# Cross-attention scores of a two-block decoder: one float32 product against three float32r products of high and low halves

## The chip, the core and the metric

The kernel runs on one core of one Trainium2 chip. The metric is the device time of one execution in microseconds (us). Work is spread over TensorE (PE: matmuls, and PEld for its weight loads), VectorE (DVE), ScalarE (ACT), GpSimd (POOL) and SyncE (SP), which issues the transfers. Each engine runs its own list of instructions in order and waits on semaphores for the others.

## The reference

256 tokens of width 1024 pass through two blocks. The first has two layers; each is a mixer (an mLSTM in the first layer, stick-breaking attention in the second), a cross-attention into 256 memory tokens and a SwiGLU network. The second block mixes three branches (hgrn, forgetting attention, attention into a second memory) and ends in a gated network with a convolution. All of it is float32. The part that the change touches is this, once in each layer:

```python
def memory_cross_attention(h, mem_n, w_q, w_kv, w_o):
    q = (h @ w_q).reshape(B, S, XA_HEADS, XA_HEAD_DIM)            # 4 heads of 256
    kv = (mem_n @ w_kv).reshape(B, mem_n.shape[1], 2, XA_HEADS, XA_HEAD_DIM)
    k, v = kv[:, :, 0], kv[:, :, 1]
    s = jnp.einsum('bthd,bmhd->bhtm', q, k).astype(jnp.float32) * (XA_HEAD_DIM ** -0.5)
    p = jax.nn.softmax(s, axis=-1).astype(v.dtype)
    o = jnp.einsum('bhtm,bmhd->bthd', p, v).reshape(B, S, D_MODEL)
    return o @ w_o
```

Two other parts of the reference play a role below. The second block normalises its memory keys by head (`kh = _rmsnorm(mk.reshape(B, M, MEM_HEADS, MEM_DH), k_g)`), and its hgrn branch needs causal masks over chunks of 64 tokens.

## The kernel before, in words

The 256 tokens are two halves h of 128 rows. Every projection (`project`, `project_T`) is already done as three float32r products: the weights are split into a high and a low half (`split_weight`: L211 on ACT casts the high half, L212 on DVE subtracts it from the raw weights to get the low half), the activations likewise (`split`: L364 on ACT, L365 on DVE), and the products hi·hi, hi·lo and lo·hi are added in PSUM (L240, L241, L244 in `prod`; L317 to L322 in `project_T`).

The cross-attention is `xattn`. Its query projection makes four blocks (h, b), h a half and b a pair of heads. Each starts a chain of its own: scale the block (L812), transpose it on PE (L354) and copy it back with the factor 1/16 on DVE (`to_T`, L383), four float32 matmuls of 128x256 against the keys (`mmf`, L388), a softmax (`softmax2`: L787 to L799), eight float32 matmuls against the values (also L388), and a split of the output. A float32 matmul appears in the profile as two records: the eight records "128x256 x8" under L388 are one chain's score products. The keys are made by `mem_kT`: a block of the key projection is copied from PSUM to SBUF on ACT (L765).

Behind the second layer's cross-attention stands work for the second block. `second_memory` projects its memory to keys and values; each half m of the keys goes through `chain_head`: `headnorm` (ACT squares, L1234; DVE sums, L1236; POOL forms the reciprocal root in four small instructions, L1237, L398, L401, L1238; DVE multiplies, L1239), then four transposes on PE (L354) and a copy (L381). So there are two head norms, one for each half. `second_consts` prepares constants; its last part is `hgrn_consts` (L1094 to L1123), which builds the seven pairs of masks on POOL out of 70 instructions: memsets (L1102, L1114), selects (L505) and casts (L1111, L1118). The order in which it is started:

```python
            self.xattn(xT, l, kT, v, y)
            if l == 1:
                self.do(lambda: self.spawn(self.second_consts()))
                mk, mv = self.second_memory(memT)
            self.out_norm(x, ng[l, 3], self.g_norm(l, 4), ins["xa_w_o"][l], y, nxt)
```

The order of instructions on each engine is fixed before the run. A plan in the kernel keeps a running estimate of PE's time (`self.pe(us)` adds to it), and a side chain that says `yield 2.2` goes on when the plan is 2.2 us later; the framework's scheduler and its tile pools then settle the order. One pool matters here: all activations of 2 KB, the mask scratch tiles too, come from `act` (`t2`, 37 buffers), and whoever takes a buffer waits for the last reader of the tile that had it before.

Of the kernel before, what the change touches and what calls it, by code (L numbers as in the profile page):

```python
# [6 lines left out]
F32 = mybir.dt.float32  # L7
F32R = mybir.dt.float32r
# [5 lines left out]
P = 128  # L14
# [6 lines left out]
MM = 0.2135  # L21
# [33 lines left out]
class Net:  # L55
# [703 lines left out]
    def mem_kT(self, memT, ap, c0, nblk):  # L759

        res = [Slot() for _ in range(2 * nblk)]

        def use(i, j, ps):
            t = self.t2([P, 2, 256])
            self.nc.scalar.copy(t, ps.rearrange("p (k t) -> p k t", k=2))  # L765
            res[2 * i + j].v = t

        self.project_T(memT, ap, [(c0 + b * 512, 512) for b in range(nblk)], use)
        return res
# [34 lines left out]
    def xattn(self, xT, l, kT, v, y):  # L804
        nc = self.nc

        def use(h, b, ps, r):
            self.spawn(chain(h, b, ps, r))

        def chain(h, b, ps, r):  # L810
            t = self.t2()
            nc.scalar.mul(t, ps, r)  # L812
            yield 1.61
            qT = self.to_T(t, 1.0 / 16.0)
            yield 2.2
            yield from self.until(*kT)
            sc = self.bank()
            for i in range(2):
                for d in range(2):
                    self.mmf(  # L820
                        sc[:, i * 256 : i * 256 + 256], qT[:, 2 * i + d, :], kT[2 * b + i].v[:, d, :],
                        d == 0, d == 1,
                    )
            pT = yield from self.softmax2(sc)
            o = self.bank()
            for i in range(2):
                for d in range(2):
                    for m in range(2):
                        self.mmf(
                            o[:, (2 * i + d) * P : (2 * i + d + 1) * P],  # L830
                            v[m][b].v[:, i * 256 + d * P : i * 256 + d * P + P], pT[:, 2 * i + m, :],
                            m == 0, m == 1,
                        )
            y[h][b].v = self.split(o)

        self.project(xT, self.ins["xa_w_q"][l], [0, 512], use)
# [918 lines left out]
```

## Time and profile before

| | |
|---|---|
| three runs, median | 1324.82 us (1323.47, 1324.82, 1325.05) |
| the profiled execution | 1324.29 us, its span 1322.5 us |
| PE busy | 1303.5 us, 99% of the span |
| DVE, ACT, POOL busy | 65%, 56%, 10% of the span |
| mean granted clock of TensorE | 0.996 |

The span runs from the first to the last instruction of the profiled execution; 1.79 us of its time lie outside it. In a timeline row the first number is the start, the second the time until the group's last instruction ended, and the bracket at the end the idle time of the engine just before, with the instruction that ended it. L12 is line 12 of the kernel.

### The profile page before, as it was taken

To read this page: it belongs to the slowest core of one execution; us is meant where nothing else is said; L and a number is where in the kernel's file an instruction comes from. 1 tells how busy PE (TensorE), PEld (TensorE's weight loads), DVE (VectorE), ACT (ScalarE), POOL (GpSimd) and SP (SyncE) were. 2 spreads that over 40 slices of the span, in tenths; PEclk is the share of its full clock that TensorE was granted. 3 is DMA by queue.
4 is the path that set the end of the run, shared out by engine and by line. 5 is a ranking of instruction groups with operands and counts; after the bars stand their busy time and mean duration, and the time that the engine had idled before them with its cause. 6 is when DMAs were issued, how large, how long until landed. Compare 5 with 4: busy or idle time off the path is not lost.

```text
span 1322.5 us, 20130 instructions
## 1 busy us (share of the span) xinstructions
PE 1303.5 (99%) x7611; PEld 1136.6 (86%) x7611; DVE 862.6 (65%) x1407; ACT 738.2 (56%) x1306; POOL 126.1 (10%) x224
## 2 busy tenths in 40 slices
PE   8999999999999999999999999998999999999998
PEld 6899888888888999887788888888998999788887
DVE  6674576756666465467585666777776666777773
ACT  6864565645556577466375555655444544656551
POOL 3000000000001000016300000012234020000000
PEclk9999999999999999999999999999899999999999
DMA  7953562655556543654365655555244456465551
GB/s 250 297 189 130 167 199 86 236 172 176 190 190 194 191 130 127 191 181 156 96 204 179 203 190 184 187 174 160 59 152 127 129 152 209 132 209 176 190 190 34
DMA packets 121435, 224.39 MB, mean 170 GB/s; under 512 B 7448, under 2 KB 19066, under 8 KB 121338
## 3 DMA queue, kind: packets, MB, share of 16 engines
q1 hardware_dynamic: 121338, 223.11, 52.6%
q8 instruction: 60, 0.98, 0.3%
q14 instruction: 37, 0.30, 0.1%
HBM read 222.03 MB, written 1.05 MB: 169 GB/s over the span
## 4 chain that ended last, share of the span: by engine, by line
PE 76%; issue 15%; DVE 3%; ACT 2%; POOL 2%; DMA 0%; POOLq 0%; DVEq 0%; ACTq 0%
PE tr L314 15%; PE mm L244 10%; PE mm L241 10%; PE mm L240 10%; PE tr L322 8%; PE tr L388 4%; PE mm L317 3%; PE mm L319 3%; PE mm L318 3%; PE tr L354 2%; DVE lo L212 1%; PE tr L244 1%; PE tr L240 1%; PE tr L241 1%; POOL s L400 1%
## 5 line engine op out<-in xcount | busy, mean ns | idle before, releaser
L212 DVE TENSOR_TENSOR lo<-raw,hi 128x1024 fp32r<-128x1024 f32 (+1 forms) x414 | 496.7, 1221 | 170.1 <-ACT hi L211 142.2
L211 ACT CAST hi<-raw 128x1024 fp32r<-128x1024 f32 (+1 forms) x414 | 423.3, 1043 | 136.7 <-PE mm L244 67.0
L240 PE MATMUL mm<-hi,t 128*128 128x512 f32 (+2 forms) x856 | 329.6, 386 | 0.0
L241 PE MATMUL mm<-lo,t 128*128 128x512 f32 (+2 forms) x856 | 327.4, 384 | 0.0
L244 PE MATMUL mm<-hi,t 128*128 128x512 f32 (+2 forms) x856 | 266.1, 386 | 0.0
L314 PE MATMUL tr<-t,hi 128*128 128x512 f32 x864 | 216.2, 392 | 0.0
L241 PEld LDWEIGHTS mm<-lo,t 128*128 128x128 f32 x856 | 161.3, 188 | 30.4 <-DVE lo L212 0.6
L240 PEld LDWEIGHTS mm<-hi,t 128*128 128x128 f32 x856 | 161.5, 189 | 29.1
L244 PEld LDWEIGHTS mm<-hi,t 128*128 128x128 f32 x856 | 158.9, 188 | 30.2
L314 PEld LDWEIGHTS tr<-t,hi 128*128 128x128 f32 x864 | 156.3, 189 | 28.6
L317 PE MATMUL mm<-t,hi 128*128 128x256 f32 x576 | 166.0, 288 | 0.0
L319 PE MATMUL mm<-t,lo 128*128 128x256 f32 x576 | 163.7, 284 | 0.0
L318 PE MATMUL mm<-t,hi 128*128 128x256 f32 x576 | 163.4, 284 | 0.0
L322 PEld LDWEIGHTS tr<-t,lo 128*128 128x128 f32 x864 | 118.0, 190 | 8.4
L322 PE MATMUL tr<-t,lo 128*128 128x256 f32 x864 | 120.9, 282 | 0.0
L317 PEld LDWEIGHTS mm<-t,hi 128*128 128x128 f32 x576 | 110.7, 192 | 2.0 <-issue 0.5
L318 PEld LDWEIGHTS mm<-t,hi 128*128 128x128 f32 x576 | 110.7, 192 | 0.8
L319 PEld LDWEIGHTS mm<-t,lo 128*128 128x128 f32 x576 | 110.8, 192 | 0.0
L400 POOL TENSOR_SCALAR s<-s 128x1 f32<-128x1 f32 x32 | 21.8, 682 | 792.5 <-ACT junk L406 791.4
L344 DVE TENSOR_TENSOR t<-tr,t 128x256 f32<-128x256 f32 x108 | 45.5, 421 | 64.5 <-ACT t L343 64.5
L388 PE MATMUL tr<-t,t 128*128 128x128 f32 (+4 forms) x672 | 83.6, 296 | 2.9 <-DVE t L1173 2.9
L388 PEld LDWEIGHTS tr<-t,t 128*128 128x128 f32 (+2 forms) x672 | 72.1, 186 | 9.0 <-POOL t L1176 2.4
(241 smaller groups left out, 1187.8 us busy)
## 6 DMA issues: line engine op xcount, KB each, us to landing
raw<-in_ffn_w_gate_up SPq DMA_DIRECT2D x88, 512.0 KB
raw<-in_ffn_w_down SPq DMA_DIRECT2D x66, 512.0 KB
raw<-in_w_in SPq DMA_DIRECT2D x54, 512.0 KB
raw<-in_ffn_w_up SPq DMA_DIRECT2D x44, 512.0 KB
raw<-in_xa_w_kv SPq DMA_DIRECT2D x32, 512.0 KB
raw<-in_sb_w_qkv SPq DMA_DIRECT2D x24, 512.0 KB
raw<-in_ml_w_in SPq DMA_DIRECT2D x22, 512.0 KB
raw<-in_xa_w_q SPq DMA_DIRECT2D x16, 512.0 KB
```

The lines of the kernel that those rows point to most:

```text
L211: self.nc.scalar.copy(hi, raw)
L212: self.nc.vector.tensor_sub(lo, raw, hi.bitcast(F32))
L240: nc.tensor.matmul(out, lhsT=a, rhs=wh, start=first and k == 0, stop=False)
L241: nc.tensor.matmul(out, lhsT=a, rhs=wl, start=False, stop=False)
L244: nc.tensor.matmul(out, lhsT=b, rhs=hl[k][0], start=False, stop=last and k == nk - 1)
L314: mm(ps, lhsT=wh, rhs=x.rearrange("p j t -> p (j t)"), start=k == 0, stop=False)
L317: mm(out, lhsT=wh, rhs=x[:, 0, :], start=k == 0, stop=False)
L318: mm(out, lhsT=wh, rhs=x[:, 1, :], start=False, stop=False)
L319: mm(out, lhsT=wl, rhs=x[:, 0, :], start=False, stop=k == kt - 1)
L322: mm(out, lhsT=wl, rhs=x[:, 0, :], start=False, stop=k == kt - 1)
L344: self.nc.vector.tensor_add(out, ps[:, 0, :], out)
L388: self.nc.tensor.matmul(out, lhsT=lhsT, rhs=rhs, start=start, stop=stop, **kw)
```

## The change

Keys and queries are split into a high and a low half of type float32r, and the scores become hi·hi + hi·lo + lo·hi, as in the projections: twelve matmuls of 128x256 for each chain in place of four in float32.

```diff
@@ mem_kT
-            t = self.t2([P, 2, 256])
-            self.nc.scalar.copy(t, ps.rearrange("p (k t) -> p k t", k=2))
-            res[2 * i + j].v = t
+            v = ps.rearrange("p (k t) -> p k t", k=2)
+            hi, lo = self.t2([P, 2, 256], F32R), self.t2([P, 2, 256], F32R)
+            self.nc.scalar.copy(hi, v)
+            self.nc.vector.tensor_sub(lo, v, hi.bitcast(F32))
+            res[2 * i + j].v = (hi, lo)
@@ xattn
             t = self.t2()
             nc.scalar.mul(t, ps, r)
             yield 1.61
-            qT = self.to_T(t, 1.0 / 16.0)
-            yield 2.2
+            qh, ql = self.split(self.transpose4(lambda j: t[:, j * P : (j + 1) * P]), scale=1.0 / 16.0)
+            yield 2.6
             yield from self.until(*kT)
             sc = self.bank()
             for i in range(2):
+                kh, kl = kT[2 * b + i].v
+                out = sc[:, i * 256 : i * 256 + 256]
                 for d in range(2):
-                    self.mmf(
-                        sc[:, i * 256 : i * 256 + 256], qT[:, 2 * i + d, :], kT[2 * b + i].v[:, d, :],
-                        d == 0, d == 1,
-                    )
+                    a = 2 * i + d
+                    nc.tensor.matmul(out, lhsT=qh[a], rhs=kh[:, d, :], start=d == 0, stop=False)
+                    nc.tensor.matmul(out, lhsT=qh[a], rhs=kl[:, d, :], start=False, stop=False)
+                    nc.tensor.matmul(out, lhsT=ql[a], rhs=kh[:, d, :], start=False, stop=d == 1)
+                    self.pe(1.5 * MM)
             pT = yield from self.softmax2(sc)
```

The function that the queries now call, `split` with a scale, was there before:

```python
    def split(self, ps, n=4, scale=None):
        hi, lo = self.t2([P, n, P], F32R), self.t2([P, n, P], F32R)
        v = ps[:, : n * P].rearrange("p (k t) -> p k t", k=n)
        ...
            nc.scalar.activation(hi, v, AF.Copy, scale=scale)
            nc.vector.scalar_tensor_tensor(lo, v, scale, hi.bitcast(F32), ALU.mult, ALU.subtract)
```

So a layer holds eight key tiles where it held four, and a chain two query tiles where it held one, all from the pool `act`. SP's list of transfers is the same before and after. On the other engines the order changes around the two cross-attentions, and outside them in one place: POOL's work behind the second layer's cross-attention. In the rows below a name is a kind of tile with its number (s: small statistics, t: a tile of the pool `act`, lv and lvm: the finished masks), and the numbers differ between the two programs.

POOL before, at the end of the mask work. The last of the 70 mask instructions are the first three rows; behind them come the first head norm's four instructions, then the second's, then a step of the output norm (L400):

```order
L1111 CAST lv1_6280<-t1380_6354 128x128 [waits Pool_49]
L505 AFFINE_SELECT t1381_6361<-t1381_6361 128x64 [waits Pool_49] x2
L1118 CAST lvm_6281<-t1381_6361 128x64 [waits Pool_49]
L1237 TENSOR_SCALAR s1388_6388<-s1388_6388 128x4 [waits DVE_49]
L398 TENSOR_SCALAR s1390_6392<-s1388_6388 128x4 [waits Pool_49]
L401 TENSOR_TENSOR s1391_6393<-s1390_6392,mhalf_112 128x4 [waits Pool_49]
L1238 TENSOR_SCALAR s1389_6389<-s1391_6393 128x4 [waits Pool_49]
L1237 TENSOR_SCALAR s1408_6457<-s1408_6457 128x4 [waits DVE_49]
L398 TENSOR_SCALAR s1410_6461<-s1408_6457 128x4 [waits Pool_49]
L401 TENSOR_TENSOR s1411_6462<-s1410_6461,mhalf_112 128x4 [waits Pool_49]
L1238 TENSOR_SCALAR s1409_6458<-s1411_6462 128x4 [waits Pool_49]
L400 TENSOR_SCALAR s1456_6654<-s1438_6592 128x1 [waits Activation_49]
```

POOL in the changed kernel, the same place. Lines from 764 on have moved down by up to five, so L1242 and L1243 are L1237 and L1238 of before, and L1107, L1116, L1119 and L1123 are the mask lines L1102, L1111, L1114 and L1118:

```order
L1242 TENSOR_SCALAR s1390_6393<-s1390_6393 128x4 [waits DVE_49]
L398 TENSOR_SCALAR s1392_6397<-s1390_6393 128x4 [waits Pool_49]
L401 TENSOR_TENSOR s1393_6398<-s1392_6397,mhalf_112 128x4 [waits PE_49,Pool_49]
L1243 TENSOR_SCALAR s1391_6394<-s1393_6398 128x4 [waits Pool_49]
L1107 MEMSET t1398_6418 128x128 [waits PE_49,Activation_49]
...
L1123 CAST lvm_6417<-t1411_6497 128x64 [waits Pool_49]
L1242 TENSOR_SCALAR s1424_6553<-s1424_6553 128x4 [waits DVE_49]
L398 TENSOR_SCALAR s1426_6557<-s1424_6553 128x4 [waits Pool_49]
L401 TENSOR_TENSOR s1427_6558<-s1426_6557,mhalf_112 128x4 [waits Pool_49]
L1243 TENSOR_SCALAR s1425_6554<-s1427_6558 128x4 [waits Pool_49]
L400 TENSOR_SCALAR s1472_6750<-s1454_6688 128x1 [waits Activation_49]
```

What has moved: the 70 mask instructions stood ahead of both head norms, and now stand between them.

PE before, where it transposes the second head norm's result (t1407). The rows around it are the value projection of the second memory (mm1424), of which two matmuls are left behind the transposes, and the first of the output projection (mm1432):

```order
L241 MATMUL mm1424_6517<-lo1338_6173,t1302_6023 128x512
L240 MATMUL mm1424_6517<-hi1337_6172,t1303_6024 128x512
L241 MATMUL mm1424_6517<-lo1338_6173,t1303_6024 128x512
L354 MATMUL tr1427_6539<-ident_114,t1407_6455 128x128 [waits DVE_49,Activation_49]
L354 MATMUL tr1427_6539<-ident_114,t1407_6455 128x128 x3
L244 MATMUL mm1424_6517<-hi1337_6172,t1302_6023 128x512
L244 MATMUL mm1424_6517<-hi1337_6172,t1303_6024 128x512
L240 MATMUL mm1432_6559<-hi1394_6406,t1311_6070 128x512 [waits Activation_49]
```

PE in the changed kernel, the same place (t1423 is the second head norm's result, mm1440 the value projection, mm1448 the output projection):

```order
L240 MATMUL mm1440_6613<-hi1347_6235,t1316_6096 128x512
L241 MATMUL mm1440_6613<-lo1348_6236,t1316_6096 128x512
L240 MATMUL mm1440_6613<-hi1347_6235,t1317_6097 128x512
L354 MATMUL tr1443_6635<-ident_114,t1423_6551 128x128 [waits DVE_49,Activation_49]
L354 MATMUL tr1443_6635<-ident_114,t1423_6551 128x128 x3
L241 MATMUL mm1440_6613<-lo1348_6236,t1317_6097 128x512
L244 MATMUL mm1440_6613<-hi1347_6235,t1316_6096 128x512
L244 MATMUL mm1440_6613<-hi1347_6235,t1317_6097 128x512
L240 MATMUL mm1448_6655<-hi1396_6411,t1325_6151 128x512 [waits Activation_49]
```

The transposes stand one matmul earlier in PE's list, and still ahead of the whole output projection.

## Rows read from the trace of the kernel before

**Rows 1.** The page: the span, the busy time of the engines, and the engines of the chain of work that ended last.

```profile
span 1322.5 us, 20130 instructions
...
PE 1303.5 (99%) x7611; PEld 1136.6 (86%) x7611; DVE 862.6 (65%) x1407; ACT 738.2 (56%) x1306; POOL 126.1 (10%) x224
...
PE 76%; issue 15%; DVE 3%; ACT 2%; POOL 2%; DMA 0%; POOLq 0%; DVEq 0%; ACTq 0%
```

**Rows 2.** Busy time of each engine in two stretches behind the second layer's cross-attention (start and end, length, then busy us and instructions for each engine, granted clock, DMA share and GB/s).

```profile
645.00:700.00 55.00, 54.85 (x261) 45.35 (x262) 39.04 (x56) 33.64 (x60) 3.96 (x8) 1.00 0.58 187
700.00:920.00 220.00, 217.79 (x1198) 189.05 (x1197) 143.84 (x220) 120.62 (x199) 13.42 (x19) 1.00 0.57 182
```

**Rows 3.** PE's timeline around one chain's scores in the first layer: the eight records of the float32 products, and the 128x512 matmuls behind them.

```profile
178.80 1.89 PE L388 MATMUL tr<-t,t 128*128 128x256 f32 x8
180.34 0.58 PE L244 MATMUL mm<-hi,t 128*128 128x512 f32 x1
180.76 0.40 PE L240 MATMUL mm<-hi,t 128*128 128x512 f32 x1
180.99 0.39 PE L241 MATMUL mm<-lo,t 128*128 128x512 f32 x1
```

**Rows 4.** PE's timeline in a projection made of float32r matmuls of 128x256, the first and the last of 15 in a row.

```profile
107.82 0.28 PE L317 MATMUL mm<-t,hi 128*128 128x256 f32 x1
...
109.49 0.28 PE L319 MATMUL mm<-t,lo 128*128 128x256 f32 x1
```

**Rows 5.** The instructions of two lines over the whole run: shortest, median and longest in ns, and where the first and the last start.

```profile
L383 DVE TENSOR_SCALAR t<-tr x8: 681/684/692, 176.2 to 626.0; 128x512 f32<-128x512 f32 x8
```

```profile
L364 ACT CAST t<-tr x20: 584/587/637, 101.4 to 695.2; 128x512 fp32r<-128x512 f32 x20
```

**Rows 6.** POOL's timeline behind the second layer's cross-attention: some rows of the mask work (606.02 to 632.92), then the two head norms.

```profile
606.02 0.20 POOL L1102 MEMSET t<- 128x128 f32 x1 [5.83 <-PE mm L244]
...
608.94 0.20 POOL L1102 MEMSET t<- 128x128 f32 x1 [2.33 <-PE tr L388]
609.11 5.35 POOL L505 TENSOR_SCALAR_AFFINE_SELECT t<-t 128x64 f32<-128x64 f32 x7
...
617.06 0.20 POOL L1102 MEMSET t<- 128x128 f32 x1 [1.26 <-PE tr L388]
...
619.58 1.22 POOL L1118 CAST lvm<-t 128x64 uint8<-128x64 f32 x1
...
621.52 2.58 POOL L505 TENSOR_SCALAR_AFFINE_SELECT t<-t 128x64 f32<-128x64 f32 x6
...
626.75 1.29 POOL L1111 CAST lv<-t 128x128 fp32r<-128x128 f32 x1
627.99 1.61 POOL L505 TENSOR_SCALAR_AFFINE_SELECT t<-t 128x64 f32<-128x64 f32 x3
...
632.92 0.24 POOL L1118 CAST lvm<-t 128x64 uint8<-128x64 f32 x1
634.63 0.25 POOL L1237 TENSOR_SCALAR s<-s 128x4 f32<-128x4 f32 x1 [1.48 <-DVE s L1236]
...
636.43 0.24 POOL L1238 TENSOR_SCALAR s<-s 128x4 f32<-128x4 f32 x1
641.38 0.23 POOL L1237 TENSOR_SCALAR s<-s 128x4 f32<-128x4 f32 x1 [4.71 <-DVE s L1236]
...
643.97 0.23 POOL L1238 TENSOR_SCALAR s<-s 128x4 f32<-128x4 f32 x1
```

**Rows 7.** DVE's timeline of the same stretch: two weight splits beside the mask work, then the head norms' work.

```profile
619.48 1.23 DVE L212 TENSOR_TENSOR lo<-raw,hi 128x1024 fp32r<-128x1024 f32 x1 [0.54 <-ACT hi L211]
...
626.70 1.20 DVE L212 TENSOR_TENSOR lo<-raw,hi 128x1024 fp32r<-128x1024 f32 x1
...
636.70 0.69 DVE L1239 TENSOR_TENSOR t<-mm,s 128x512 f32<-128x512 f32 x1 [2.16 <-POOL s L1238]
...
640.62 0.68 DVE L1236 TENSOR_REDUCE s<-t 128x4 f32<-128x512 f32 x1
641.44 1.23 DVE L212 TENSOR_TENSOR lo<-raw,hi 128x1024 fp32r<-128x1024 f32 x1
644.23 0.69 DVE L1239 TENSOR_TENSOR t<-mm,s 128x512 f32<-128x512 f32 x1 [1.56 <-POOL s L1238]
```

**Rows 8.** PE's timeline at the second head norm's transposes, and at an earlier wait for a query chain in the same layer.

```profile
602.90 0.65 PE L354 MATMUL tr<-ident,t 128*128 128x128 f32 x4 [1.12 <-DVE t L383]
...
643.30 0.39 PE L241 MATMUL mm<-lo,t 128*128 128x512 f32 x1
645.07 0.63 PE L354 MATMUL tr<-ident,t 128*128 128x128 f32 x4 [1.38 <-DVE t L1239]
645.45 0.70 PE L244 MATMUL mm<-hi,t 128*128 128x512 f32 x2
```

**Rows 9.** Busy time of each engine in four stretches where the granted clock (third number from the end) changes; the columns are those of rows 2.

```profile
8.30:11.70 3.40, 3.40 (x9) 2.32 (x8) 2.65 (x5) 2.99 (x6) 0.00 (x0) 0.52 1.05 397
11.70:15.10 3.40, 3.40 (x18) 2.83 (x17) 1.92 (x5) 1.68 (x6) 0.00 (x0) 1.00 1.05 379
```

```profile
922.00:926.00 4.00, 2.22 (x17) 1.81 (x16) 4.00 (x7) 0.93 (x3) 1.66 (x1) 1.00 0.45 126
926.30:933.10 6.80, 6.44 (x29) 6.47 (x30) 4.16 (x15) 0.60 (x1) 3.72 (x9) 0.50 0.26 77
```

## The prediction, made before the changed kernel ran

> **What bounds the kernel now.** The page comes first: PE is busy for 1303.5 of the span's 1322.5 us, and three quarters of the chain that ended last are PE's own instructions [rows 1]. So a change is worth what it does to PE: the time of PE's instructions, and the waits it puts in front of them. Then the stretches behind the second layer's cross-attention, where the change also moves work: PE is busy for 54.85 of 55 us, and for 217.79 of the next 220 [rows 2]. There is next to no idle time in which PE could make up for a delay. A delay of PE there ends up whole in the time.
>
> **The arithmetic on PE.** One chain's four float32 products are eight records from 178.80. The 128x512 matmul behind them is ready for its successor at 180.76, and such matmuls follow each other every 0.23 us (180.76 to 180.99), so the block takes 180.53 − 178.80 = 1.73 us [rows 3]. The twelve float32r matmuls that replace it have the same 256 columns as a projection's, where the 15 rows from 107.82 to 109.49 are 14 steps of 0.119 us [rows 4]; twelve take 1.44 us. The gain is 0.29 us for a chain, and with eight chains 2.3 us, half in each layer.
>
> A page speaks of the same matmuls. The Trainium skill, TensorE: Matmul & The Clock Gate, Back-to-back issue gap, gives an isolated gap of columns/2.4 + 2.5 ns, 109 ns for 256 columns. By that twelve take an estimated 1.31 us and the eight chains gain 3.4 us; the row of 0.119 us decides here, since it stands in the same sort of stream, weight loads included.
>
> **The splits on ACT and DVE.** A query copy on DVE of 0.684 us becomes an ACT cast like L364's, 0.587 us, and a DVE subtraction of about the size of the old copy [rows 5]. A key copy on ACT becomes that pair too, so in all eight casts go to ACT and eight subtractions to DVE. In busy time this is hidden, since DVE stands at 65% and ACT at 56% [rows 1]. What it can cost is latency: the queries come some 0.6 us later to the scores. PE has other matmuls to do meanwhile, and before, this chain delayed it once, by 1.12 us at 602.90 [rows 8]. At that place in the second layer one weight split more (L212, 1.23 us [rows 7]) now stands ahead of a chain's subtraction on DVE. I count 1.1 us against the gain, and keep 0 and 2.3 us as bounds: nothing where other matmuls cover it, the whole gain where each of two such places costs 1.2.
>
> **What is moved: the masks.** Before, POOL does the 70 mask instructions from 606.02 to 633.16, is then idle until the first head norm's sum is there (1.48 us behind DVE), and has that head norm's four instructions done at 636.67 [rows 6]. The second head norm comes at 641.38, after 4.71 us of idling. In the changed order those 70 instructions stand between the two. Their own waits name PE and ACT, and each is for something that those engines do ahead of the first head norm, so nothing holds the masks back once POOL reaches them, but also nothing starts them earlier. The second head norm stands behind all of them.
>
> How long do they take? From 606.02 to 633.16 it is 27.1 us; waits inside are 2.33 and 1.26 us, and another 0.2 at the second memset, which leaves 23.3 [rows 6]. Some of them were slow. The cast L1118 takes 1.22 us at 619.58 and 0.24 at 632.92; at 619.48 DVE starts a weight split of 1.23 us. The cast at 626.75 takes 1.29, with a split on DVE at 626.70 [rows 6, 7]. From the starts of the instructions I count six that were long in this way, two among the selects of 609.11, one each in the groups at 621.52 and 627.99 and these two casts, by 0.55 to 1.0 us each, 5.0 together. Undisturbed the masks would take 18.3 us. In the new place DVE has one split (that of 641.44) ahead of the second head norm's multiplication, so I add 0.9 for one long instruction: 19.2 us. Behind that split DVE itself waits, and can disturb no more. The bounds are 18.3 and 23.3.
>
> The Trainium skill says the same of such a pair: SBUF — State Buffer, Who interferes with whom, has a VectorE instruction with two SBUF inputs (the weight split is one) contend with a GpSimd instruction that reads SBUF, the later one blocked until the other ends. By that rule a DVE that stands still leaves the masks at full speed; by the trace's sum alone, without it, they would take 23.3 us and the result would be 4.1 us later.
>
> **The sum at the second head norm.**
> - First head norm on POOL: 634.63, less the 1.2 us net gain up to there, 633.4; its four instructions take 636.67 − 634.63 = 2.04, so 635.5.
> - Masks: 19.2, so 654.7.
> - Second head norm on POOL: the same 2.04, so 656.7. (Before it took 2.8, beside a split.)
> - DVE's multiplication follows 0.03 later. Before, from its start at 644.23 to PE's transposes at 645.07 it was 0.84 us, and 0.38 more to the next projection matmul at 645.45 [rows 7, 8]. So PE goes on with the projection at 658.0.
> - Before, that was 645.45: 12.5 us. PE then has three matmuls left of the projection where it had two, 0.23 more: 12.8 us.
>
> This already contains every gain and loss on the way, for it compares the same point of the work. PE itself would have been there at about 643.7 − 1.2 (its wait of 1.38 us before ended at 645.07 [rows 8]), so it stands still for about 15 us. In that time DVE, in its own order, stands behind the multiplication, and PE behind DVE; the four transposes stand in front of the end of the value projection and of the whole output projection, so nothing else can run.
>
> **What is late next.** After the stall DVE has some four weight splits of 1.2 us and two copies of 0.7 to do, while the halves needed first by the output projection were split before; PE has over 6 us of such matmuls. I cost that at 0; without this cover it would be up to 2 us. The granted clock does cost something. At the start, the stretch from 8.30 to 11.70 has a granted clock of 0.52, that is near 1.2 GHz, with 9 matmuls, and the next 3.40 us at 1.00, 2.4 GHz, have 18: 1.7 us lost. Behind a stretch in which PE was busy for only 2.22 of 4 us, 926.30 to 933.10 runs at 0.50, so 3.4 us lost [rows 9]. PE will have done nothing for 15 us. I take 1.7, with 0 and 3.4 as bounds.
>
> Sum, on the profiled execution's own time: 1324.29 + 12.8 + 1.7 = **1338.8 us**. That execution lies 0.5 us under the median of the runs, which changes nothing at this size.
>
> **The rivals.**
> - *The masks don't hold up the second head norm* (the other side). Place: POOL behind the first head norm. Then only the arithmetic is left: 1324.29 − 2.3 = 1322.0 us; if the query chains cost nothing. For it speaks that POOL is busy for only 10% [rows 1] and that before it idled for 4.71 us in just this place [rows 6]. It decides at the masks' length: PE is there at about 642.5, and needs 2.0 + 0.9 us from POOL's first step to its transposes, so the masks would have to be done by 639.6, in 4.1 us in place of 18 to 23. Against it: 70 instructions in 4.1 us are 59 ns each, and the shortest rows shown take 200. Chance 0.06.
> - *The gain is eaten by the queries' latency, and the masks hide as well*: 1322.0 + 2.3 = 1324.3 us. The 1.12 us wait speaks for the first half; the second has the same case against it as above. Chance 0.05.
> - *Masks as slow as before and a long low clock*: DVE's splits disturb the masks as they did (23.3 in place of 19.2), and the clock costs 3.4: 1324.29 + 12.8 + 4.1 + 3.4 = 1344.6 us. Against it: DVE stands still for most of the time. Chance 0.12.
> - *The stall without any loss of clock, and the whole arithmetic gain ahead of it*: 1324.29 + 12.8 − 1.1 − 0.9 = 1335.1 us. Chance 0.15.
> - The forecast, 1336 to 1342 us: 0.62.
>
> **Numbers.** The range reaches from the fourth rival to the third, with a little for what the sum leaves out at either end (2 us of backlog, 2 us caught up of the idle time in rows 2): 1333 to 1346 us. A measurement of this kernel can tell about 0.2%, 2.6 us, from no change. Faster by more than that needs the first rival with more than its 2.3 us: 0.04. Within it lie the rest of the first rival and the second: 0.07. Slower: 0.89.
>
> **What would show it.** In the changed kernel's POOL timeline the first head norm stands near 633, then the masks without a gap for 18 to 20 us, then the second head norm near 655. PE's transposes there show an idle time of about 15 us put down to DVE's multiplication, and DVE before it one of some 13 us put down to POOL. The granted clock falls to about 0.5 behind the stall for a few us. The scores appear as twelve rows 0.12 us apart. Behind that the stretches of rows 2 take as long as before, only later. The prediction is wrong if the masks run in some other place or in a few us, if PE's transposes don't wait, or if the time comes back further down.

## The result, and the profile after

The changed kernel takes 1339.42 us (median of four runs, 1337.9 to 1340.13) against 1324.93 us before; the ratio is 1.0112, 95% interval 1.0099 to 1.0125. It is slower by 14.5 us, and the forecast was 1338.8 in a range of 1333 to 1346. The page of the changed kernel, the lines that answer to [rows 1]:

```profile
span 1336.2 us, 20215 instructions
...
PE 1303.5 (98%) x7643; PEld 1136.6 (85%) x7643; DVE 866.7 (65%) x1415; ACT 742.7 (56%) x1314; POOL 119.6 (9%) x224
...
PE 61%; issue 27%; DVE 4%; POOL 4%; ACT 2%; DMA 1%; SPq 0%; POOLq 0%; DVEq 0%; ACTq 0%
```

PE is busy for as long as before, 1303.5 us, in a span 13.7 us longer. So what was added is waiting. POOL's busy time even fell, from 126.1 to 119.6 us: the loss isn't more work on POOL but work in another place. POOL's timeline of the changed kernel shows it, to be held against [rows 6] (L1242 and L1243 are the head norm's first and last step, L1107 to L1123 and the selects of L505 the masks):

```profile
633.89 0.25 POOL L1242 TENSOR_SCALAR s<-s 128x4 f32<-128x4 f32 x1 [33.12 <-DVE s L1241]
...
635.68 0.24 POOL L1243 TENSOR_SCALAR s<-s 128x4 f32<-128x4 f32 x1
635.86 0.20 POOL L1107 MEMSET t<- 128x128 f32 x1
...
641.80 1.93 POOL L505 TENSOR_SCALAR_AFFINE_SELECT t<-t 128x64 f32<-128x64 f32 x3
...
654.21 0.24 POOL L1123 CAST lvm<-t 128x64 uint8<-128x64 f32 x1
654.40 0.23 POOL L1242 TENSOR_SCALAR s<-s 128x4 f32<-128x4 f32 x1
...
656.17 0.23 POOL L1243 TENSOR_SCALAR s<-s 128x4 f32<-128x4 f32 x1
```

From 635.86 to 654.45 the masks run without a gap, 18.6 us, and the second head norm starts right behind them with no idle time. DVE's timeline (first fence) and PE's (second) show who stands behind them, to be held against [rows 7, 8]:

```profile
637.16 0.68 DVE L1241 TENSOR_REDUCE s<-t 128x4 f32<-128x512 f32 x1
642.15 1.36 DVE L212 TENSOR_TENSOR lo<-raw,hi 128x1024 fp32r<-128x1024 f32 x1 [4.32 <-ACT hi L211]
656.43 0.69 DVE L1244 TENSOR_TENSOR t<-mm,s 128x512 f32<-128x512 f32 x1 [12.92 <-POOL s L1243]
```

```profile
644.04 0.39 PE L240 MATMUL mm<-hi,t 128*128 128x512 f32 x1
657.27 1.09 PE L354 MATMUL tr<-ident,t 128*128 128x128 f32 x4 [12.84 <-DVE t L1244]
658.01 0.78 PE L241 MATMUL mm<-lo,t 128*128 128x512 f32 x1
...
661.99 0.57 PE L240 MATMUL mm<-hi,t 128*128 128x512 f32 x1
662.40 0.40 PE L241 MATMUL mm<-lo,t 128*128 128x512 f32 x1
```

The sum that the multiplication needs (L1241) was ready at 637.84; POOL took it up at 654.40. DVE idles 12.92 us for POOL and PE 12.84 us for DVE. Busy time in four stretches, in the columns of [rows 2]:

```profile
645.00:658.00 13.00, 0.73 (x4) 0.76 (x5) 1.57 (x3) 0.33 (x1) 11.01 (x51) 0.64 0.10 36
658.00:662.00 4.00, 4.00 (x12) 3.13 (x11) 3.81 (x4) 1.55 (x2) 0.00 (x0) 0.50 0.48 132
...
670.00:715.00 45.00, 44.91 (x218) 37.17 (x217) 34.30 (x50) 31.40 (x56) 3.99 (x8) 1.00 0.57 187
715.00:935.00 220.00, 217.80 (x1199) 189.17 (x1198) 143.43 (x220) 120.85 (x199) 13.48 (x19) 1.00 0.57 182
```

For 13 us hardly anything but POOL works. PE resumes at a granted clock of 0.50, the lower of its two levels, until 662. Behind that the work runs as before: 217.80 of 220 us busy where it was 217.79. Nothing is made up.

### The profile page after: what moved, and what is told of

It is laid out like the page before. It is cut to its first block, busy times and chain, and to the rows that moved or that the text cites. A ratio compares the mean times of both kernels' runs of the same rounds, so it can differ in the third digit from the quotient of the medians.

```text
span 1336.2 us, 20215 instructions
## 1 busy us (share of the span) xinstructions
PE 1303.5 (98%) x7643; PEld 1136.6 (85%) x7643; DVE 866.7 (65%) x1415; ACT 742.7 (56%) x1314; POOL 119.6 (9%) x224
## 4 chain that ended last, share of the span: by engine, by line
PE 61%; issue 27%; DVE 4%; POOL 4%; ACT 2%; DMA 1%; SPq 0%; POOLq 0%; DVEq 0%; ACTq 0%
PE tr L314 10%; PE mm L244 9%; PE mm L241 9%; PE mm L240 9%; PE tr L322 5%; PE mm L317 3%; PE mm L318 3%; PE mm L319 3%; PE tr L388 3%; PE tr L354 2%; DVE lo L212 2%; POOL t L505 1%; PE tr L244 1%; POOL s L400 1%; PE tr L241 1%
## 5 line engine op out<-in xcount | busy, mean ns | idle before, releaser
L400 POOL TENSOR_SCALAR s<-s 128x1 f32<-128x1 f32 x32 | 21.3, 665 | 796.1 <-ACT junk L406 777.5
L343 ACT COPY t<-tr 128x256 f32<-128x256 f32 x108 | 39.6, 368 | 56.8 <-PE tr L322 55.9
L354 PE MATMUL tr<-ident,t 128*128 128x128 f32 x328 | 49.8, 278 | 21.6 <-DVE t L1244 14.1
```

What stands on the lines that cost most here:

```text
L354: self.nc.tensor.transpose(ps[:, i * P : (i + 1) * P], src(i), self.ident)
```

## The experiments

The theory: the whole loss comes from POOL's 70 mask instructions, which stand between the two head norms; the three products gain a little. The rival: the splits of keys and queries, on the way to the scores, or the products themselves cost the time. One line of the change belongs to neither: `yield 2.6` in place of `yield 2.2`, which lets the plan take up the query chain 0.4 us later. The first two kernels test whether this number moves the masks.

**One number put back in the changed kernel.**

```diff
             qh, ql = self.split(...)
-            yield 2.6
+            yield 2.2
```

> The changed kernel with one number put back: the query chain says yield 2.2 where the change says yield 2.6. In its program the 70 mask instructions stand ahead of both head norms again; arithmetic and splits are those of the changed kernel. If the masks between the two head norms are the loss: PE's wait for the second head norm's multiplication is 0 to 1.5 us in place of 12.8, and the time is 1322.0 to 1325.0 us (1324.9, less 2.3 of arithmetic, plus 0 to 2.3 of latency of the query chains). If the splits and the three products are the loss: the time stays at 1338 to 1341 us, since all of them are still there.

Measured: 1327.37 us, ratio to before 1.0024 (1.0015 to 1.0033). The masks are back ahead of both head norms and 12 of the 14.5 us are gone, with all splits and products in place, so the rival is out as the cause of the main loss. But the time is 2.4 us above the range that I gave. POOL's timeline of this kernel, and then a row of PE's:

```profile
620.67 0.21 POOL L1107 MEMSET t<- 128x128 f32 x1 [20.09 <-DVE t L368]
...
641.82 0.24 POOL L1123 CAST lvm<-t 128x64 uint8<-128x64 f32 x1
642.03 0.25 POOL L1242 TENSOR_SCALAR s<-s 128x4 f32<-128x4 f32 x1
```

```profile
644.92 0.63 PE L354 MATMUL tr<-ident,t 128*128 128x128 f32 x4 [3.88 <-DVE t L1244]
```

The masks start at 620.67, not at 606.02 as before [rows 6], and now it is the first head norm that waits for their end: PE stands for 3.88 us. So there is a second effect of the change, which the first had covered. Where it comes from is tested below, under more tiles.

**That number alone in the kernel before.**

```diff
             qT = self.to_T(t, 1.0 / 16.0)
-            yield 2.2
+            yield 2.6
```

> The kernel before with that one number alone: yield 2.6 in place of 2.2, scores still in float32. In its program the masks stand between the two head norms, as in the changed kernel. If the masks' place is the loss: POOL does them from about 636 to 655, PE waits 12 to 15 us there, and the time is 1338.5 to 1342.5 us (1324.9 + 12.8 + 1.7 to 3.4, without the gain of the arithmetic). If the splits and products are the loss: 1324 to 1326 us.

Measured: 1335.9 us, ratio 1.0090 (1.0076 to 1.0103). Without a single split or product changed, one number of the plan gives most of the loss. POOL's timeline, then PE's:

```profile
631.49 0.25 POOL L1237 TENSOR_SCALAR s<-s 128x4 f32<-128x4 f32 x1 [31.54 <-DVE s L1236]
...
633.46 0.20 POOL L1102 MEMSET t<- 128x128 f32 x1
...
651.20 0.23 POOL L1237 TENSOR_SCALAR s<-s 128x4 f32<-128x4 f32 x1
```

```profile
654.06 1.08 PE L354 MATMUL tr<-ident,t 128*128 128x128 f32 x4 [12.26 <-DVE t L1239]
```

The time is 2.6 us under my range. The first head norm comes 3.1 us earlier than before (631.49 against 634.63 [rows 6]); I had taken its time from the kernel before, but the number moves the chain ahead of it too. And the masks take 17.7 us, since no weight split falls beside them.

**The masks later, in the changed kernel and in the kernel before.** In both, the masks go to the feed-forward network behind:

```diff
             nc.gpsimd.tensor_copy(masks[:, l, :], m)
+            yield 12.0
...
             yield 0.5
-        self.hgrn_consts()
+        yield 40.0
+        yield from self.hgrn_consts()
```

> The changed kernel (yield 2.6) with the masks made later: 40 us of the plan after the other constants, and with 12 us of the plan between the seven levels, so that they stand among POOL's work of the feed-forward network. If the masks' place is the loss: no wait of PE for a head norm above 1 us, and 1320.5 to 1324.0 us. If POOL's work there takes the place of the old wait (a level of masks ahead of a step of an output norm, up to 3.6 us each): up to 1328 us. If the splits and products are the loss: 1338 to 1341 us.

> The kernel before with the masks made later in the same way. Beside the run above it gives the change alone, without the masks on either side. The head norm's wait of 1.4 us may go with the masks' interference: 1323.0 to 1325.5 us. The difference of the two: the run above is 2.3 us faster if the arithmetic comes through whole, 0 to 1 us faster if the later queries take it back, and slower if the splits cost more than the products save.

Measured: 1323.35 us for the changed kernel, ratio 0.9993 (0.9984 to 1.0002), and 1324.21 us for the kernel before, 0.9999 (0.9990 to 1.0008). So with yield 2.6, splits and products all in place, the 14.5 us are gone when the masks stand elsewhere. PE's longest wait for a head norm in the changed kernel with later masks:

```profile
PE tr L354 <- DVE t L1245: 1.3, 1, 1.3
```

That is a little over the 1 us that I had allowed, and the kernel before with later masks keeps 1.4 us there.

The change by itself, read from the two medians, is worth 0.9 us, not 2.3, and that lies within the intervals. The section on the prediction says where the rest went.

**The masks in buffers of their own, in both.**

```diff
-        self.act = pool(name="act", bufs=37)
+        self.act = pool(name="act", bufs=36)
...
+        self.msk = pool(name="msk", bufs=2)
...
-            f = self.t2([P, P])
+            f = self.msk.tile([P, P], F32, tag="f", name=self.name("f"))
...
-            m = self.t2([P, P // 2])
+            m = self.msk.tile([P, P // 2], F32, tag="m", name=self.name("m"))
```

> The changed kernel (yield 2.6) with scratch buffers of their own for the masks (two for each of the two shapes), paid for with one buffer of the large pool, 36 in place of 37. In its program the 70 mask instructions now stand at the front of POOL's list, for nothing there waits for a buffer any more. If the shared buffers and the place of the masks are the loss: no mask instruction after 600 us, PE's wait for a head norm 0 to 1.5 us, 1321.5 to 1324.5 us. If one buffer less costs PE waits elsewhere: above that, up to 1330. If the splits and products are the loss: 1338 to 1341 us.

> The kernel before with the masks' own buffers and 36 in the large pool. 1322.5 to 1325.0 us. Beside the run above it is a second reading of the change without the masks: 2.3 us faster for the three products if nothing takes the gain back; 0 to 1 us, as in the two runs with later masks (1323.35 and 1324.21), if the later queries do.

Measured: 1327.87 us, 1.0031 (1.0020 to 1.0043), and 1328.33 us, 1.0034 (1.0021 to 1.0046). Both missed the ranges, by the same mechanism at another place. The masks, free of any wait, now stand at the front of POOL's list, from 1.80 on, ahead of constants that the first layer needs. POOL's timeline of the changed kernel with own buffers (the last mask, and the first of those constants, L530; from L78 on each line number is one higher here than in the changed kernel), then a row of DVE's timeline and one of PE's waits (us in total, times, longest):

```profile
23.18 0.24 POOL L1124 CAST lvm<-m 128x64 uint8<-128x64 f32 x1
23.35 0.34 POOL L530 MEMSET t<- 128x128 f32 x2
```

```profile
23.98 0.34 DVE L534 CAST nls<-t 128x128 fp32r<-128x128 f32 x1 [5.93 <-POOL t L506]
```

```profile
PE mm L245 <- DVE t L460: 5.3, 1, 5.3
```

In the kernel before with own buffers this wait is 6.4 us; with shared buffers neither has it. DVE idles 5.93 us for those constants, which POOL makes from 1.81 on in the changed kernel and from 23.35 on here; PE's wait comes behind that in DVE's list. This was read from the order and the waits, and was not tested by an edit of its own. The difference of the two medians, 0.46 us, is the second reading of the change alone.

**More tiles, in the kernel before.** Every key and query block copied twice, and both copies read by the scores:

```diff
             self.nc.scalar.copy(t, ps.rearrange("p (k t) -> p k t", k=2))
-            res[2 * i + j].v = t
+            u = self.t2([P, 2, 256])
+            self.nc.vector.tensor_copy(u, ps.rearrange("p (k t) -> p k t", k=2))
+            res[2 * i + j].v = (t, u)
...
-                        qT[:, 2 * i + d, :], kT[2 * b + i].v[:, d, :],
+                        qT[d][:, 2 * i + d, :], kT[2 * b + i].v[d][:, d, :],
```

> The kernel before, yield 2.2 and float32 scores, but with as many tiles as the changed kernel: every key block and every query block is copied twice, by ACT and by DVE, and the scores read one copy for the first 128 rows of a head and the other for the rest. If the tiles delay the masks (the buffers come free later): the first mask instruction starts near 620 in place of 606, the first head norm waits behind the masks, PE waits 3 to 5 us for its multiplication, and the time is 1326 to 1329.5 us, like the changed kernel with yield 2.2 (1327.4) and a little more, for there the products were cheaper. If that delay came from the splits' latency or the products: masks from about 606, 1324 to 1326 us.

Measured: 1330.74 us, 1.0049 (1.0035 to 1.0063). POOL's timeline, and its row of PE's waits:

```profile
621.53 0.20 POOL L1108 MEMSET t<- 128x128 f32 x1 [20.30 <-PE tr L388]
...
643.28 0.25 POOL L1243 TENSOR_SCALAR s<-s 128x4 f32<-128x4 f32 x1
```

```profile
PE tr L354 <- DVE t L1245: 3.5, 1, 3.5
```

The masks start at 621.53, and PE waits 3.5 us, as in the changed kernel with yield 2.2 (620.67 and 3.88): the tiles and their copies, with float32 scores, do it. The buffers in which the masks are drawn now come free only when a chain's scores (L388) have read them. This kernel also has a wait of 1.95 us for a query's copy at 605.07, and no cheaper products. The time is 1.2 us above my range, and the profile shows what I hadn't counted: the granted clock falls behind each of these two waits. Two stretches in the columns of [rows 2]:

```profile
606.16:609.57 3.41, 3.41 (x10) 2.66 (x9) 3.41 (x13) 1.31 (x6) 0.00 (x0) 0.50 0.84 279
...
647.12:650.53 3.41, 3.41 (x10) 2.63 (x9) 2.36 (x4) 2.04 (x2) 1.91 (x4) 0.50 0.02 4
```

At half the clock each costs some 1.7 us; the kernel before has 1.00 in both places. The profile of the changed kernel with yield 2.2 has two such stretches too, from 604.78 and from 645.74.

**The masks twice.**

```diff
-        for l in range(7):
+        for l in [l for l in range(7) for _ in range(2)]:
```

> The changed kernel with every mask made twice, 140 mask instructions between the two head norms in place of 70. If PE stands behind POOL there with no slack: the wait of 12.8 us grows by the masks' 18.3 to 18.7 us to about 31.3, and the time is 1339.4 + 18.3 to 18.7, 1357 to 1359 us. If another wait would have ended almost as late: less than that. If the granted clock loses more after a longer stall: up to 1.7 us more.

Measured: 1352.46 us, 1.0214 (1.0195 to 1.0232): 13.0 us above the changed kernel, or 14.0 when each is taken against the runs of the kernel before beside it, and less than the 18.3 to 18.7 expected. POOL's timeline, then PE's:

```profile
634.83 0.20 POOL L1107 MEMSET t<- 128x128 f32 x1
...
672.86 0.22 POOL L1242 TENSOR_SCALAR s<-s 128x4 f32<-128x4 f32 x1
```

```profile
675.71 1.09 PE L354 MATMUL tr<-ident,t 128*128 128x128 f32 x4 [26.89 <-DVE t L1244]
```

The masks take 38.0 us in place of 18.6, POOL starts them 1.0 earlier, and DVE's multiplication comes 18.4 us later (674.87 against 656.43), as it must if nothing else would have held it. But PE's wait grew by only 14.05. With twice the masks in the plan the scheduler put the four transposes 24 matmuls further down in PE's list (55 behind the first head norm's transposes in place of 31). At 0.23 us each these are 5.5 us of work, and less the 1.0 us of the earlier start they cover 4.4 us of the longer stall: PE arrives at 648.82 where it arrived at 644.43. The expectation failed on a program that I took to be otherwise the same.

**The second head norm without POOL.** The masks stay where the change has put them, and the second head norm's factor is formed on DVE, without the square root:

```diff
-        nc.gpsimd.tensor_scalar(ms, ms, 1.0 / dh, None, ALU.mult)
-        nc.gpsimd.tensor_scalar(f, self.rstd(ms), r, None, ALU.mult)
+        if dve:
+            e = self.small(nh)
+            nc.vector.tensor_scalar(e, ms, 1.0 / dh, EPS, ALU.mult, ALU.add)
+            nc.vector.reciprocal(f, e)
+            nc.vector.tensor_scalar(f, f, r, None, ALU.mult)
+        else:
+            nc.gpsimd.tensor_scalar(ms, ms, 1.0 / dh, None, ALU.mult)
+            nc.gpsimd.tensor_scalar(f, self.rstd(ms), r, None, ALU.mult)
...
-            self.spawn(self.chain_head(ps, r, 4, mk[m]))
+            self.spawn(self.chain_head(ps, r, 4, mk[m], dve=m == 1))
```

> The changed kernel (yield 2.6, masks behind the first head norm), with the second head norm's four POOL instructions replaced by three on DVE: scale and epsilon, reciprocal, factor. The square root of that step is left out, so the second half of the second memory's keys is scaled by another number; nothing else differs. The masks stay where they are, right behind the first head norm. If POOL's list is all that holds up the second head norm: the masks still run from about 636 to 654, PE's wait for the multiplication is 0 to 1.5 us in place of 12.8, the granted clock stays at 1.00 there, and the time is 1322.5 to 1326 us. If DVE or PE wait there for something else as well (the tiles' buffers, the weight splits): 1330 us or more.

Measured: 1322.59 us, 0.9994 (0.9984 to 1.0003). POOL's timeline, DVE's second head norm, and two stretches in the columns of [rows 2]:

```profile
634.43 0.20 POOL L1107 MEMSET t<- 128x128 f32 x1
...
655.85 0.24 POOL L1123 CAST lvm<-t 128x64 uint8<-128x64 f32 x1
```

```profile
643.21 0.68 DVE L1250 TENSOR_TENSOR t<-mm,s 128x512 f32<-128x512 f32 x1
```

```profile
645.00:658.00 13.00, 13.00 (x59) 10.75 (x58) 4.65 (x7) 3.16 (x7) 11.83 (x49) 1.00 0.40 122
658.00:662.00 4.00, 4.00 (x19) 3.32 (x18) 3.15 (x4) 3.97 (x9) 1.27 (x2) 1.00 0.22 61
```

POOL works from 634.43 to 656.09 as in the changed kernel, longer even, for four weight splits now fall beside the masks. But DVE multiplies at 643.21 in place of 656.43, PE is busy for 13.00 of the 13 us in which it had been busy for 0.73, and the granted clock stays at 1.00. So it is neither the masks' work nor a lack of buffers that costs the time, but that the second head norm stood behind them in POOL's list.

**Later masks with yield 2.2.** The kernel with later masks, and the query chain's number put back as in the first run.

> The changed kernel with later masks and yield 2.2 in place of 2.6. If the number matters only through the masks' place: the same as with 2.6 (1323.35), within 0.1%. If the queries' chain is better started earlier or later: the difference shows what the number is worth by itself, 0.5 to 2 us either way.

Measured: 1323.05 us, 0.9995 (0.9987 to 1.0004), against 1323.35 with yield 2.6. By itself the number is worth nothing that can be measured; it matters through the masks' place alone.

No version beats the kernel before clear of the noise: the three best, 1322.59, 1323.05 and 1323.35 us, all have 1.0 inside their intervals.

## The prediction, point by point

- **The bound.** Right. PE's busy time is the same to 0.1 us, the loss is idle time of PE, and the stretches behind it are as full as before.
- **The masks' place and length.** Right: 18.6 us where 19.2 were worked out. The one select that is long, in the group at 641.80, stands beside the one weight split of the stretch, at 642.15. Other runs fill in the scale, with POOL's waits inside the masks taken off: 17.7 us with no split beside them, 20.8, 21.3 and 21.7 with four, 23.3 before with six. My undisturbed 18.3 was 0.6 too much; 0.8 to 1 us for each split is what these runs show. The Trainium skill, SBUF — State Buffer, Who interferes with whom, fits that: by it the later of the two instructions waits. The cast at 619.58 does, with 1.22 us in place of 0.24, behind the split at 619.48 [rows 6, 7].
- **The sum at the second head norm.** The next projection matmul was to come at 658.0, and came at 658.01. That is better than its terms, and so partly luck. The first head norm on POOL was to start at 633.4 and started at 633.89; the masks and the small steps around them were shorter by 0.8; and the four transposes, at the lower clock, took 0.74 us in place of 0.38.
- **PE's stall.** The mechanism was right, the size off: 12.84 us where I had about 15. I let PE arrive at about 642.5; it arrived at 644.43, mainly because the gain on the way was 0.7 us and not 1.2, and PE had waited 1.28 us for the first head norm too. It changes nothing in the sum, since the end of the stall is set by POOL.
- **The clock.** 1.7 us were taken, with 0 and 3.4 as bounds. From 657.27 to 662.40 PE did four transposes and ten matmuls, which take 0.38 + 10 × 0.23 = 2.7 us at the upper level [rows 8]; it took 5.1. So the loss was 2.4 us, 0.7 more than taken. At 662.40 the changed kernel is 14.8 us behind the same matmul of the kernel before, and 14.6 still at 939.61. At the end it is 13.7, and as far as these runs show that is chance: before, a stretch of 6.8 us at 0.50 began at 926.30 [rows 9], which the changed kernel's profile doesn't have at that point of its work. There PE waits instead, so of the 3.4 us that I read from that stretch only 0.9 come back:

```profile
945.71 0.28 PE L319 MATMUL mm<-t,lo 128*128 128x256 f32 x1
947.72 0.41 PE L354 MATMUL tr<-ident,t 128*128 128x128 f32 x2 [1.72 <-DVE t L383]
```

  Near 28 us it is the other way round: the changed kernel's profile has a stretch of 3.41 us at 0.50 there that the profile of before doesn't have, worth some 1.5 us. The profiled execution is also the fastest of the four, 1337.9 us; the others have a lower mean granted clock (0.990 and 0.991 against 0.993). So the total, 0.6 us under the median, agrees more closely than its terms do.
- **The arithmetic.** A little too large. PE's timeline in the second layer, the first, the second and the eleventh of a chain's twelve, and what follows the twelfth; from the second on the steps are 0.119 us, as in [rows 4]:

```profile
605.29 0.36 PE L825 MATMUL tr<-t,t 128*128 128x256 f32 x1
605.49 0.28 PE L826 MATMUL tr<-t,t 128*128 128x256 f32 x1
...
606.56 0.28 PE L826 MATMUL tr<-t,t 128*128 128x256 f32 x1
...
606.80 0.40 PE L240 MATMUL mm<-hi,t 128*128 128x512 f32 x1
```

  The step from the first to the second is 0.20 us, and in six of the eight chains it is about that. [Rows 4] leave such a step out: three matmuls ahead of its first one it is 0.21 us too. So the eight chains' twelve take 12.1 us from start to start, not 11.5, and the products save 8 × 1.73 − 12.1 = 1.7 us in place of 2.3.
- Of that gain less comes through: without the masks it is 0.9 and 0.5 us by two pairs of kernels, neither clear of zero. Most of what is missing is the term that I had named, the later queries. DVE's timeline of the changed kernel, then PE's, at the place of the 1.12 us wait of [rows 8]:

```profile
601.60 2.35 DVE L212 TENSOR_TENSOR lo<-raw,hi 128x1024 fp32r<-128x1024 f32 x2
603.87 0.68 DVE L368 SCALAR_TENSOR_TENSOR t<-tr,t 128x512 fp32r<-128x512 f32 x1
```

```profile
604.61 0.66 PE L354 MATMUL tr<-ident,t 128*128 128x128 f32 x4 [1.98 <-DVE t L368]
```

  Two weight splits, not one, stand ahead of the queries' subtraction, and PE waits 1.98 us: 0.9 more than before, where I had counted 1.1. That leaves 0.8 us, which these runs don't tell from the two readings. The figure of the Trainium skill (TensorE: Matmul & The Clock Gate, Back-to-back issue gap), 109 ns for such a gap, differs from the 119 that the rows show here too; the rows decide.
- **What is late next.** Right that it costs nothing: DVE's splits behind the stall were done by 662, and PE had no wait there.
- **The rivals.** The other-side one, the arithmetic alone, was given 1322.0 us, and the kernel comes near it once the second head norm is off POOL's list: 1322.59, though the kernel before took 1323.85 beside it, so 1.3 us were gained and not 2.3. The one with the long clock loss and slow masks, 1344.6, fell: DVE did stand still. The one without any loss of clock, 1335.1, fell by the 2.4 us. Of the one with the queries' latency the first half came true, in part; the masks did not hide.
- **What I had not seen.** The change has a second cost in its tiles: even with the masks in their old order it would have lost some 3 us, since the masks' buffers come free 15 us later. It was hidden behind the larger one, and no term or rival of the prediction had it. In the two profiles that show it the granted clock is low behind the shorter waits as well.

## What to carry to other kernels

A change's cost can lie in what it does to the order of work that it doesn't touch: here one number of a plan, worth nothing by itself, moved 18.6 us of idle-engine work between two short steps, of which the second is on the path of the bounding engine. So read the program's order on every engine before and after, the quiet ones first, and ask of each long run of instructions that has moved what now stands behind it. And test such a loss by moving that work elsewhere with the change left in place; but look at the new order too, since one such move, the masks' own buffers, put a stall at the start of the run.

## What the runs showed of the hardware

POOL's 70 mask instructions took 17.7 and 18.6 us with none and one of DVE's weight splits beside them, 20.8, 21.3 and 21.7 with four, and 23.3 with six. After 12.84 us without work PE resumed at a granted clock of 0.50 for 5.1 us; after 26.89 us without work, in the run with twice the masks, the first 5.00 us were at 0.50 and the next 3.30 at 0.86 on average, so about 5.9 us at the lower level: a stall twice as long lengthened the slow stretch by only 0.8 us. Shorter waits can be followed by the lower clock too: in the run with more tiles there are 3.41 us at 0.50 behind the wait of 1.95 us, and as much behind that of 3.5 us. It isn't certain: behind the 1.98 us before 604.61 the changed kernel's clock stayed at 1.00. The start of a run varies too: the changed kernel's profile has a short stretch at the lower clock near 28 us, worth some 1.5 us, where the one of before has it near 8 us [rows 9], and some of the variants have neither. Why it falls there was not tested.
